# One level of Strassen's scheme for the three large products of a gated block

## The chip, the core and the metric

The kernel runs on one core of a Trainium2 chip. The metric is device time in microseconds (us), from the first to the last instruction of the program on that core. Five engines work side by side, each with its own queue of instructions in a fixed order: PE (TensorE, matrix products), DVE (VectorE), ACT (ScalarE), POOL (GpSimd) and SP (SyncE, which here issues DMAs). They wait for each other through semaphores. SBUF is the on-chip memory, PSUM the small memory into which PE accumulates, and DRAM is off the chip.

## The reference

One layer on 1024 positions and 2048 channels, all in float32:

```python
hn = rmsnorm(h, pre_g[l])
z = hn @ w_in[l]                                   # 2048 -> 5120
u, v, gate_a, xb, gate_b = jnp.split(z, splits, axis=-1)
ya = gmlp_branch(u, v, ...) * jax.nn.silu(gate_a)  # gelu(u) * (mix over positions of layernorm(gelu(v)))
yb = rglru_branch(xb, ...) * jax.nn.silu(gate_b)   # conv of width 4, two small gates, a linear recurrence
y = jnp.concatenate([rmsnorm(ya, gmlp_out_g[l]), rmsnorm(yb, lru_out_g[l])], axis=-1)
h = h + rmsnorm(y @ w_out[l], post_g[l])           # 2048 -> 2048
h = h + (p[l] @ w_pe[l]) * jax.nn.sigmoid(h @ w_pg[l])   # 2048 -> 2048
```

The three large products are those with `w_in`, `w_out` and `w_pg`.

## The kernel before

Channels lie on the 128 partitions and positions along the free axis. A float32 product is done as three passes of a shorter type, float32r: `split` (L71 to L79) makes of each operand a head (a rounding copy on ACT) and a rest (source minus head on DVE), and PE adds head by head, rest of the weights by head of the activations, and head of the weights by rest of the activations into one PSUM tile. Every full matmul has 128 x 128 weights and 512 positions.

`load_w` (L81) brings a tile of 128 x 512 weights from DRAM over SP's queue and splits it. `block` (L109) makes one block of 128 output channels: 16 blocks of K, three passes, two halves of the positions, so 96 matmuls into a PSUM tile of two banks. `group` (L155) does several blocks together, block of K by block of K, while the activations of a phase are still being made (`Stream`, L133). The activations of a phase stay in SBUF, split, for the whole phase (the pool `t4` of 47 tiles).

The phases are: A, the input projection (first three blocks of xb and gate_b in one `group`, then the recurrent branch `lru` block by block; the v blocks with positions on the partitions, L388 to L404; then u and gate_a); B, the output projection (`evac_o`, L481), whose result goes to DRAM; C, the residual sum and the gate product (`make_half`, L544, `finish`, L614). Before C the last block of B is done one half of the positions after the other (`block_by_cuts`, L119): the norm of the first half (`o_rms`, `o_spread`) stands in PE's order in the middle of the second half's products, and the first three blocks of C begin with the first half of six blocks of K (`early_h`, `N_STAGED`).

The code is recorded in the order of the text, and a scheduler then sets each engine's order by its own model of times. Counted in the built program, PE has 7218 matmuls' worth of 128 x 512 (two of 256 columns counted as one), beside some hundred small ones.

## Time and profile before

| | |
|---|---|
| median of 3 runs | 1708.62 us (1707.32 to 1708.95) |
| span of the profiled execution | 1707.4 us |
| PE, matmuls | 1679.2 us (98%) |
| PE, weight loads | 1383.9 us (81%) |
| DVE | 681.7 us (40%) |
| ACT | 493.0 us (29%) |
| POOL | 194.6 us (11%) |
| DMA | 139.67 MB, mean 82 GB/s |

A busy share is a mean over the span. What an engine that is idle on average costs is seen only in the stretch in which it is needed most, so the trace is also read by stretches of time. The granted clock is 1.00 where PE runs at 2.4 GHz and 0.50 at 1.2 GHz; a mean between them is a stretch with both.

### The profile page before, as it was taken

How to read it: one execution, taken by the hardware profiler on the slowest of the kernel's cores; microseconds unless marked ns; L12 is line 12 of the kernel's file. 1: busy time of each engine (PE TensorE's matmuls, PEld its weight loads, DVE VectorE, ACT ScalarE, POOL GpSimd, SP SyncE). 2: the span in 40 equal slices, each digit the busy share in tenths (PEclk: the TensorE clock that was granted, in tenths of full speed). 3: DMA queues.
4: the chain of work that ended last, by engine and by line, in shares of the span. 5: the costliest groups of instructions: out<-in, count | busy, mean ns of one | idle time of the engine just before them, and what ended most of it. 6: DMA issues, size and time to landing. Idle time of an engine off the chain costs nothing. (4 is left out here: it accounts for less than half of the span.)

```text
span 1707.4 us, 18341 instructions
## 1 busy us (share of the span) xinstructions
PE 1679.2 (98%) x7476; PEld 1383.9 (81%) x7476; DVE 681.7 (40%) x830; ACT 493.0 (29%) x666; POOL 194.6 (11%) x99
## 2 busy tenths in 40 slices
PE   7999999999999999999999999999999899999999
PEld 5888888888888888888888888888887588888887
DVE  7775455455343332222225731111118952221221
ACT  5554333345333222222223421111113321111110
POOL 5500000001000000000000111111111741111000
PEclk9999999999999999999999999999999999999999
DMA  6221111113323211111114032222237322221220
GB/s 219 91 72 53 65 65 62 64 60 117 87 80 99 78 40 50 50 49 46 48 50 147 21 109 71 73 74 74 74 124 275 134 93 74 75 76 57 74 75 25
DMA packets 66468, 139.67 MB, mean 82 GB/s; under 512 B 7376, under 2 KB 11600, under 8 KB 66384
## 3 DMA queue, kind: packets, MB, share of 16 engines
q1 hardware_dynamic: 60768, 118.52, 21.3%
q10 hardware_dynamic: 5616, 19.99, 3.0%
q8 instruction: 58, 0.95, 0.2%
q14 instruction: 26, 0.21, 0.0%
HBM read 118.03 MB, written 20.45 MB: 81 GB/s over the span
## 5 line engine op out<-in xcount | busy, mean ns | idle before, releaser
L106 PE MATMUL z<-xah,w_hl 128*128 128x512 f32 x2048 | 551.0, 392 | 11.7 <-ACT xah L77 7.9
L75 DVE TENSOR_TENSOR w_hl<-w_raw,w_hl 128x512 fp32r<-128x512 f32 (+2 forms) x339 | 259.2, 771 | 696.9 <-ACT w_hl L74 696.8
L74 ACT ACTIVATE w_hl<-w_raw 128x512 fp32r<-128x512 f32 (+2 forms) x339 | 206.9, 616 | 940.9 <-PE z L106 756.1
L106 PEld LDWEIGHTS z<-xah,w_hl 128*128 128x128 f32 x2048 | 385.9, 189 | 95.0 <-ACT xah L77 8.8
L106 PE MATMUL z<-xal,w_hl 128*128 128x512 f32 x1024 | 312.0, 391 | 0.0
L106 PE MATMUL z<-yah,w_hl 128*128 128x512 f32 x1024 | 272.2, 390 | 1.4 <-ACT yah L77 0.9
L106 PEld LDWEIGHTS z<-yah,w_hl 128*128 128x128 f32 x1024 | 191.9, 188 | 42.0 <-ACT yah L77 1.3
L106 PEld LDWEIGHTS z<-xal,w_hl 128*128 128x128 f32 x1024 | 193.0, 189 | 40.3
L106 PE MATMUL z<-hah,w_hl 128*128 128x512 f32 (+1 forms) x660 | 172.3, 385 | 5.0 <-DVE w_hl L75 5.0
L106 PE MATMUL z<-yal,w_hl 128*128 128x512 f32 x512 | 155.3, 389 | 0.0
L106 PEld LDWEIGHTS z<-hah,w_hl 128*128 128x128 f32 x660 | 123.0, 189 | 30.6 <-DVE w_hl L75 6.3
L106 PE MATMUL z<-hh,w_hl 128*128 128x512 f32 (+1 forms) x594 | 135.9, 386 | 2.8 <-ACT hh L74 2.8
L106 PEld LDWEIGHTS z<-hh,w_hl 128*128 128x128 f32 x594 | 110.1, 190 | 25.4 <-ACT hh L74 3.4
L106 PEld LDWEIGHTS z<-yal,w_hl 128*128 128x128 f32 x512 | 96.1, 188 | 20.0
L106 PE MATMUL z<-hal,w_hl 128*128 128x512 f32 (+1 forms) x330 | 101.8, 390 | 2.9 <-DVE hal L75 2.7
L397 PE MATMUL z<-w_hl,xah 128*128 128x512 f32 x256 | 100.0, 392 | 0.0
L399 PE MATMUL z<-w_hl,xal 128*128 128x512 f32 x256 | 99.8, 390 | 0.0
L398 PE MATMUL z<-w_hl,xah 128*128 128x512 f32 x256 | 99.8, 390 | 0.0
L231 POOL TENSOR_TENSOR acca<-acca,u 128x1024 f32<-128x1024 f32 x7 | 18.8, 2692 | 512.3 <-ACT u L230 512.3
L106 PEld LDWEIGHTS z<-hal,w_hl 128*128 128x128 f32 x330 | 62.4, 191 | 18.1 <-DVE hal L75 6.2
L231 POOL TENSOR_TENSOR acco<-acco,oq 128x1024 f32<-128x1024 f32 x14 | 33.6, 2398 | 288.8 <-ACT oq L230 288.8
L398 PEld LDWEIGHTS z<-w_hl,xah 128*128 128x128 f32 x256 | 48.1, 188 | 10.1 <-issue 0.2
(168 smaller groups left out, 1190.6 us busy)
## 6 DMA issues: line engine op xcount, KB each, us to landing
w_raw<-w_z SPq DMA_DIRECT2D x125, 256.0 KB, 3.0
w_raw<-w_v SPq DMA_DIRECT2D x64, 256.0 KB, 2.6
w_raw<-w_o SPq DMA_DIRECT2D x64, 256.0 KB, 3.1
w_raw<-w_g SPq DMA_DIRECT2D x64, 256.0 KB, 3.0
xr<-xT SPq DMA_DIRECT2D x25, 512.0 KB, 7.7
o_d<-o ACTq DMA_DIRECT2D x15, 512.0 KB, 2.9
outT<-sg ACTq DMA_DIRECT2D x15, 512.0 KB, 3.3
or<-o_d SPq DMA_DIRECT2D x9, 512.0 KB, 10.2
```

The source lines that it names most:

```text
L74: nc.scalar.activation(out=hi, in_=src, func=AF.Copy)
L75: nc.vector.tensor_tensor(out=lo, in0=src, in1=hi.bitcast(F32), op=ALU.subtract)
L106: nc.tensor.matmul(ps[:, c], lhsT=hl[:, w, j * P:(j + 1) * P], rhs=a[x][:, c], start=first and n == 0, stop=last and n == 2)
L231: nc.gpsimd.tensor_tensor(out=acc, in0=acc, in1=tmp, op=ALU.add)
L397: nc.tensor.matmul(ps, lhsT=xh, rhs=hl[:, 0], start=k == 0, stop=False)
L398: nc.tensor.matmul(ps, lhsT=xh, rhs=hl[:, 1], start=False, stop=False)
L399: nc.tensor.matmul(ps, lhsT=xl, rhs=hl[:, 0], start=False, stop=k == NK - 1)
```

## The change

Each of the products is cut in two along the output channels, the channels summed over, and the positions, and one level of Strassen's scheme (in Winograd's form) is used: seven products of half-size blocks in place of eight. A unit is a pair of blocks of 128 output channels (xb with gate_b, u with gate_a, the two halves of the output channels of B and C, and four units of v); a product of a unit ("a run") takes 8 blocks of K, three passes and 512 positions: 24 matmuls. There are 36 units, so 36 x 7 x 24 = 6048 matmuls of 128 x 512 where 6912 stood.

The seven products are done in two sets. Set 1 (`set1`) needs the activation quarters 11 and 21 and the sums T1 and T2; set 2 (`set2`) needs T3, T4 and quarter 22. All act tiles of one set fill the pool of activations (`N_ACT = 32` tiles), so a phase does set 1 for all units, then set 2. What set 2 still needs of set 1 goes to DRAM as partial sums (`u2`, `u4`, `c11`, `p7`, ...) and comes back. Normalised activations go to DRAM too (`xn_d`, `yn_d`, `h_d`) and are loaded again for each sum in which they stand (`fetch_x`, `fetch_y`, `fetch_h`) into a ring of four tiles (`t_ld`, `N_LD = 4`). The norm of x is now applied to x before the product. The product with `w_pe` moves to the start of the program, where x is loaded.

Units go through a set in groups of n = 1, 2 or 4 (the tuples `L1`, `U1`, `B1`, ...), each block of weights being split whole (128 x 1024). Weight sums are made on DVE and POOL from the raw tiles (`t_raw`, five of them). `load_late` makes a DMA wait for the first matmul of the run before the last recorded one.

```diff
+L1 = (1, 1, 1, 1, 4)
+ONES8 = (1,) * 8
+U1 = (2, 1, 1, 1, 1, 2)
+B1 = (4, 4)
+B2 = (2, 1, 1, 1, 1, 2)
+C1 = (4, 4)
+C2 = (2, 1, 1, 1, 1, 1, 1)
...
+    def load_late(out, src, back=2):
+        ins = load.dma_start(out=out, in_=src)
+        if len(marks) >= back:
+            tc.add_manual_dep(ins.ins, marks[-back].ins.name,
...
+        def t12(self, c):
...
+            x11, x12 = self.fetch(0, c), self.fetch(1, c)
+            sub(x11, x12, x11)
+            x22 = self.fetch(3, c)
+            sub(x22, x22, x11)
+            self.put("T2", c, x22)
+            self.put("T1", c, x11)
...
+        def t34(self, c):
...
+            x12, x22 = self.fetch(1, c), self.fetch(3, c)
+            sub(x12, x22, x12)
+            if ("T3", c) not in self.made:
+                self.put("T3", c, x12)
+            self.put("22", c, x22)
+            x11, x21 = self.fetch(0, c), self.fetch(2, c)
+            sub(x21, x21, x11)
+            sub(x21, x21, x12)
+            self.put("T4", c, x21)
...
+            for j in tiles:
+                for c in self.chunks(j):
+                    self.acts.t12(c)
+                x11 = a11[j] if self.n == 1 else self.raw(0, j)
+                a21, a22 = self.raw(2, j), self.raw(3, j)
+                add(a21, a21, a22)
+                sub(a22, a21, x11)
+                self.run(pa, "T2", self.hl(a22), j, False)
...
+            s3, a22 = [], []
+            for j in tiles:
+                for c in self.chunks(j):
+                    self.acts.t3(c)
+                a11, a21 = self.raw(0, j), self.raw(2, j)
+                sub(a11, a11, a21)
+                s3.append(a11)
+                self.run(pa, "T3", self.hl(a11), j)
+            self.each(p7, pa)
+            for j in tiles:
+                for c in self.chunks(j):
+                    self.acts.t34(c)
+                a22.append(self.raw(3, j))
+                self.run(pa, "T4", self.hl(a22[-1]), j, False)
+            self.each(p74, pa)
+            pb = [psum() for _ in tiles]
+            for j in tiles:
+                a12 = self.raw(1, j)
+                sub(a12, a12, a22[j], nc.gpsimd)
+                add(a12, a12, s3[j])
+                self.run(pb, "22", self.hl(a12), j)
+            self.each(p3, pb)
...
+    def fetch_h(q, c):
+        t = t_ld("h")
+        if (q, c) in normed_h:
+            load_late(t, h_d[q][c])
+            return t
+        normed_h.add((q, c))
+        i, j = q // 2, q % 2
+        x = t_ld("x2")
+        load_late(x, xq[q, c])
+        load_late(t, o_d[q][c])
+        for e in range(2):
+            nc.vector.scalar_tensor_tensor(out=t[:, e], in0=t[:, e],
+                                           scalar=col("post_g", 8 * i + 2 * c + e),
+                                           in1=s_o[j], op0=ALU.mult, op1=ALU.mult)
+        add(t, t, x, nc.gpsimd)
+        store.dma_start(out=h_d[q][c], in_=t)
+        return t
...
+    for j in range(2):
+        s_o[j] = norm_half([acco[:, HALF[j]], *last_sq[j]], D, "s_o", j)
```

What moves in the engines' orders is seen at three places.

PE in the recurrent stage, before: L106 is a block product (`xah`, `xal` are head and rest of the activations), L336 the small gate products of `lru`. A block's 96 matmuls end in a PSUM tile of its own, and the next block has another.

```order
L106 MATMUL z<-xah,w_hl 128x512 x2
L336 MATMUL g<-xcl,wgs 128x512 x2
L336 MATMUL g<-xch,wgs 128x512 x2
L106 MATMUL z<-xah,w_hl 128x512 x2
L106 MATMUL z<-xal,w_hl 128x512 x2
L106 MATMUL z<-xah,w_hl 128x512 x4
L106 MATMUL z<-xal,w_hl 128x512
```

PE in the recurrent stage, after: the end of a run with T3, then four matmuls of the run with quarter 22 (`a22h`, `a22l`), then the run with T4, which adds into the PSUM tile that T3 filled and that has been read in between.

```order
L282 MATMUL z<-aT3h,w_hl 128x512 x2
L282 MATMUL z<-aT3l,w_hl 128x512
L282 MATMUL z<-a22h,w_hl 128x512 x2
L282 MATMUL z<-a22l,w_hl 128x512
L282 MATMUL z<-a22h,w_hl 128x512
L282 MATMUL z<-aT4h,w_hl 128x512 x2
L282 MATMUL z<-aT4l,w_hl 128x512
```

Between the reading of T3's sum and the first matmul of T4 there are now four matmuls of other work; before, no product went back into a tile that had been read.

PE between B and C, before: L199 sums squares over the partitions, L216 spreads the norm's scale; both stand among products (`yah` of B's last block, `hh` of C's first blocks).

```order
L106 MATMUL z<-hh,w_hl 128x512 x27
L199 MATMUL g<-ones_r,oq 128x1
L199 MATMUL g<-ones_r,acco 128x1
L199 MATMUL g<-ones_r,oq 128x1
L199 MATMUL g<-ones_r,acco 128x1
L199 MATMUL g<-ones_r,oq 128x1
L199 MATMUL g<-ones_r,acco 128x1
L199 MATMUL g<-ones_r,oq 128x1
L106 MATMUL z<-hh,w_hl 128x512 x21
L216 MATMUL g<-diag,ones_r 128x512 x2
L106 MATMUL z<-hh,w_hl 128x512 x54
```

PE between B and C, after: L155 and L172 do the same work, for the first half of the positions and then for the second, and the products of C (`a11h`) come behind both.

```order
L172 MATMUL g<-diag,ones_r 128x512 x2
L155 MATMUL g<-ones_r,acco 128x1
L155 MATMUL g<-ones_r,sq 128x1 x4
L155 MATMUL g<-ones_r,acco 128x1
L155 MATMUL g<-ones_r,sq 128x1 x4
L155 MATMUL g<-ones_r,acco 128x1
L155 MATMUL g<-ones_r,sq 128x1 x4
L155 MATMUL g<-ones_r,acco 128x1
L155 MATMUL g<-ones_r,sq 128x1 x4
L172 MATMUL g<-diag,ones_r 128x512 x2
L282 MATMUL z<-a11h,w_hl 128x512 x8
```

No block product stands between the two halves' norms any more; the same pattern stands ahead of U1 and of B.

DVE at the beginning of C, before (halves of 512 positions: scale L545, sum L548, rest L75):

```order
L545 SCALAR_TENSOR_TENSOR xo<-xo,cv,g 128x512 x2
L548 TENSOR_TENSOR xo<-xo 128x512 x2
L545 SCALAR_TENSOR_TENSOR xo<-xo,cv,g 128x512
L75 TENSOR_TENSOR hh<-xo,hh 128x512 x2
L548 TENSOR_TENSOR xo<-xo 128x512
L545 SCALAR_TENSOR_TENSOR xo<-xo,cv,g 128x512 x2
L75 TENSOR_TENSOR hh<-xo,hh 128x512
```

DVE in set 1 of C, after, from the T1 and T2 sums of the first four units (L877 scales o, L121 is a difference or a rest):

```order
L877 SCALAR_TENSOR_TENSOR h<-h,cv,s_o 128x512 x2
L121 TENSOR_TENSOR h<-h 128x1024
L121 TENSOR_TENSOR w_hl<-w_raw,w_hl 128x1024
L877 SCALAR_TENSOR_TENSOR h<-h,cv,s_o 128x512 x2
L121 TENSOR_TENSOR w_hl<-w_raw,w_hl 128x1024
L121 TENSOR_TENSOR h<-h 128x1024
L121 TENSOR_TENSOR aT2l<-h,aT2h 128x1024
L121 TENSOR_TENSOR aT1l<-h,aT1h 128x1024
```

This stands there for each of four chunks of K, beside the weight sums; the sum of x and o between L877 and L121 moved to POOL (16 additions of 128 x 1024).

## Rows read from the trace of the kernel before

**Rows 1.** The page, busy time of each engine, share and instructions.
```profile
PE 1679.2 (98%) x7476; PEld 1383.9 (81%) x7476; DVE 681.7 (40%) x830; ACT 493.0 (29%) x666; POOL 194.6 (11%) x99
```

**Rows 2.** Stretches: us, busy (instructions) PE, PEld, DVE, ACT, POOL, granted clock, DMA share, GB/s.
```profile
0.00:24.00 24.00, 16.12 (x59) 12.44 (x60) 16.25 (x41) 14.17 (x20) 7.39 (x9) 1.00 0.76 260
100.00:300.00 200.00, 200.00 (x879) 164.18 (x878) 105.00 (x106) 89.80 (x110) 9.65 (x4) 1.00 0.20 66
```

**Rows 3.** Groups by shape: out<-in, shapes, count | busy us, mean ns | idle before, releasers.
```profile
L231 POOL TENSOR_TENSOR acco<-acco,oq 128x1024 f32<-128x1024 f32 x14 | 33.6, 2398 | 288.8 <-ACT oq L230 288.8
...
L352 DVE TENSOR_TENSOR_SCAN q<-r,i 128x1024 f32<-128x1024 f32 x8 | 18.3, 2288 | 0.2
...
L462 ACT ACT_TABLE_LOAD x8 | 10.3, 1283 | 9.4 <-DVE u L309 9.3
...
L75 DVE TENSOR_TENSOR xcl<-xc,xch 128x1024 fp32r<-128x1024 f32 x8 | 9.8, 1220 | 1.4 <-ACT xch L74 1.3
...
L545 DVE SCALAR_TENSOR_TENSOR xo<-xo,cv,g 128x512 f32<-128x512 f32 x12 | 8.6, 743 | 2.3 <-PE g L216 2.3
...
L74 ACT ACTIVATE xch<-xc 128x1024 fp32r<-128x1024 f32 x8 | 8.4, 1047 | 3.7 <-DVE xc L319 3.7
...
L548 DVE TENSOR_TENSOR xo<-xo 128x512 f32<-128x512 f32 x12 | 7.9, 685 | 0.0
```

**Rows 4.** Timeline near the start: start us, us, engine, line, operation, tiles.
```profile
23.34 9.34 POOL L231 TENSOR_TENSOR accx<-accx,xr 128x1024 f32<-128x1024 f32 x3
...
27.62 6.21 DVE L75 TENSOR_TENSOR w_hl<-w_raw,w_hl 128x512 fp32r<-128x512 f32 x3
...
34.95 0.68 DVE L75 TENSOR_TENSOR w_hl<-w_raw,w_hl 128x512 fp32r<-128x512 f32 x1
```

**Rows 5.** Timeline of the second norm before C, and DVE after it.
```profile
1296.51 0.58 ACT L503 ACTIVATE oq<-z 128x512 f32<-128x512 f32 x1
...
1297.72 0.28 PE L199 MATMUL g<-ones_r,oq 128*128 128x1 f32 x2
...
1301.73 0.69 DVE L214 TENSOR_TENSOR diag<-ident,sp_lo 128x512 fp32r<-128x512 f32 x1
...
1313.51 0.68 DVE L75 TENSOR_TENSOR hh<-xo,hh 128x512 fp32r<-128x512 f32 x1
1314.11 0.69 DVE L548 TENSOR_TENSOR xo<-xo 128x512 f32<-128x512 f32 x1
```

**Rows 6.** Stretches of the step from B to C, columns as in Rows 2.
```profile
1300.00:1310.00 10.00, 7.24 (x27) 5.62 (x26) 7.29 (x16) 1.59 (x4) 0.00 (x0) 0.87 1.04 398
...
1320.00:1330.00 10.00, 8.83 (x38) 6.54 (x36) 10.00 (x10) 3.53 (x7) 7.82 (x5) 1.00 1.03 409
...
1350.00:1360.00 10.00, 4.96 (x15) 3.07 (x15) 10.00 (x8) 2.18 (x4) 8.66 (x6) 0.76 0.29 93
```

**Rows 7.** DMA issues: tensors, queue, count, KB each, median us to landing.
```profile
w_raw<-w_z SPq DMA_DIRECT2D x125, 256.0 KB, 3.0
...
xr<-xT SPq DMA_DIRECT2D x25, 512.0 KB, 7.7
...
or<-o_d SPq DMA_DIRECT2D x9, 512.0 KB, 10.2
...
pr<-pT SPq DMA_DIRECT2D x2, 512.0 KB, 6.3
```

More of the change, by code (lines that the diff above doesn't have):

```diff
@@ new lines, in groups, with __init__, p1, p2 @@
+    def groups(w, sizes, acts):
+        at = 0
+        for n in sizes:
+            yield at, Group(w[at:at + n], n, acts)
+            at += n
+    class First1:
+        def __init__(self, d, at, done, turned=False):
+            self.d, self.at, self.done, self.t = d, at, done, {}
+        def p1(self, u, ps):
+            self.t[u, 1] = t_h("c11")
+            copy(self.t[u, 1], ps)
+        def p2(self, u, ps):
+            t = self.t[u, 1]
+            add(t, t, ps)
+            self.done(self.at + u, t)
+        def u2(self, u, ps):
+            self.t[u, 2] = t_h("u2")
+            copy(self.t[u, 2], ps)
+            store.dma_start(out=self.d[self.at + u]["u2"], in_=self.t[u, 2])
+        def u4(self, u, ps, b):
+            t = t_h("u4")
+            if b is None:
+                copy(t, ps)
+            else:
+                add(t, self.t[u, 2], b)
+            store.dma_start(out=self.d[self.at + u]["u4"], in_=t)
+        def run(self, group):
+            group.set1(self.p1, self.p2, self.u2, self.u4)
@@ new lines, in block_kernel @@
+    for n in range(4):
+        if n:
+            we_raw.append(t_raw())
+            load.dma_start(out=we_raw[n], in_=w_e[n])
+        for qc in order[6 * n:6 * n + 6]:
+            load_x(*qc)
+        hl = pool.tile([P, 2, T], F32R, tag="hl", bufs=N_HL, name="w_hl")
+        split(hl[:, 0], hl[:, 1], we_raw[n])
+        for qc in order[6 * n:6 * n + 6]:
+            square_x(*qc)
+        if n == 3:
+            norm_x()
+        for b in range(4 * n, 4 * n + 4):
+            pss = [psum(), psum()]
+            for k in range(2):
+                o = ((b - 4 * n) * 2 + k) * P
+                for i, (w, x) in enumerate(((0, 0), (1, 0), (0, 1))):
+                    for j, ps in enumerate(pss):
+                        nc.tensor.matmul(ps, lhsT=hl[:, w, o:o + P], rhs=pa[k][x][:, j],
+                                         start=k == 0 and i == 0, stop=k == 1 and i == 2)
+            for j, ps in enumerate(pss):
+                t = t_h("pe")
+                copy(t, ps)
+                store.dma_start(out=pe_d[b % 8][:, 2 * (b // 8) + j], in_=t)
@@ new lines, in block_kernel, with fetch_y @@
+    ax3 = Acts(fetch_x)
+    for at, g in groups(w_u1, U1, ax3):
+        ls = [LastU(at + n) for n in range(g.n)]
+        each = [lambda n, *a, k=k: getattr(ls[n], k)(n, *a) for k in ("p1", "p2", "u2", "u4")]
+        g.set1(*each)
+    s_a = {}
+    normed = set()
+    def fetch_y(q, c):
+        t = t_ld("y")
+        if (q, c) in normed:
+            load_late(t, yn_d[q][c])
+            return t
+        normed.add((q, c))
+        load_late(t, y_d[q][c])
+        i, j = q // 2, q % 2
+        s = s_a[j] if i else s_b[j]
+        for e in range(2):
+            nc.vector.scalar_tensor_tensor(out=t[:, e], in0=t[:, e],
+                                           scalar=col("gmlp_out_g" if i else "lru_out_g", 2 * c + e),
+                                           in1=s, op0=ALU.mult, op1=ALU.mult)
+        store.dma_start(out=yn_d[q][c], in_=t)
+        return t
@@ new lines, in block_kernel, with done_o @@
+    acca = acc
+    acc = cpool.tile([P, T], F32, tag="acco", name="acco")
+    o_u = parts("ou", NH, ("u2", "u4"))
+    started = set()
+    def done_o(u, q, t, last=None):
+        store.dma_start(out=o_d[q][u // 2][:, u % 2], in_=t)
+        j = q % 2
+        if last is not None:
+            sq = t_h("sq")
+            nc.scalar.activation(out=sq, in_=t, func=AF.Square)
+            last.setdefault(j, []).append(sq)
+            return
+        add_sq(acc[:, HALF[j]], t, j not in started)
+        started.add(j)
@@ new lines, in block_kernel, with done_z @@
+    acco = acc
+    z_u = parts("zu", NH, ("u2", "u4"))
+    def done_z(u, q, t):
+        ph = t_ld("ph")
+        load_late(ph[:, 0], pe_d[u][:, q])
+        load_late(ph[:, 1], h_d[q][u // 2][:, u % 2])
+        nc.scalar.activation(out=t, in_=t, func=AF.Sigmoid)
+        mul(t, t, ph[:, 0])
+        add(t, t, ph[:, 1])
+        store.dma_start(out=outq[q, u], in_=t)
+    for j in range(2):
+        s_o[j] = norm_half([acco[:, HALF[j]], *last_sq[j]], D, "s_o", j)
+    ah1 = Acts(fetch_h)
+    for at, g in groups(w_g1, C1, ah1):
+        First1(z_u, at, lambda u, t: done_z(u, 0, t)).run(g)
@@ L644 @@
+    ah2 = Acts(fetch_h)
+    for at, g in groups(w_g2, C2, ah2):
+        Last2(z_u, at, g.n, done_z).run(g)
 def kernel(**inputs):
```

942 lines of the change are left out of this document (493 added, 449 removed).

## The prediction

> **What bounds the kernel now.** I read the busy row of the page first: PE is busy for 1679.2 of 1707.4 us, DVE for 681.7, ACT for 493.0, POOL for 194.6 [rows 1]. The whole idle time of PE is 28.2 us, at the start and at the step from B to C [rows 2, 6]. So the time is the number of matmuls times their pace, and nothing else is worth much by itself. The pace is seen in a stretch without a hole: 879 matmuls in 200 us [rows 2], 0.2275 us each at full clock. The other engines have slack on the mean, but the change spends just that slack, so the second reading is what their operations cost: a DVE operation on two tiles of 128 x 1024 takes 1.22 us, on 512 columns 0.685, a scaling of 512 columns 0.743, the same sum on POOL 2.4, a copy on ACT 1.05 and a change of ACT's function table 1.28 [rows 3]. The third is whether DVE and POOL can work at once: near the start POOL makes three sums in 9.34 us, and in the same time three DVE operations that take 0.68 alone take 6.21 together [rows 4]. From 27.62 to 33.83 us there are 2.0 us of DVE's own work and two POOL sums of 2.4: they add up to 6.8 of the 6.2 us. Where both read two SBUF tiles I therefore add DVE's and POOL's times instead of taking the longer.
>
> **What it removes.** Of 6912 block matmuls 6048 stay; 864 x 0.2275 = 196.6 us of PE. PE's own work after is 1679.2 - 196.6 = **1482.6 us** (the product with `w_pe`, the gates and the norms are in it as before). This is the floor; before's idle 28.2 us are replaced by the terms below. A run of 24 matmuls is 5.46 us.
>
> **What it adds.** Weight rests go from 4 to 7 per unit of 128 x 1024, with four weight sums on DVE and one on POOL; over the program DVE comes to some 1100 us by these rows and POOL to some 210. On the mean that fits under PE; by stretches it doesn't always. ACT comes to some 850 us (256 weight copies of 1.05, 79 table loads, 285 DMA issues); no stretch is bound by it beside the start.
>
> *Start, +22.* PE begins with the product with `w_pe`: half a MB of p lands in 6.3 us [rows 7] and is copied, so at about 8.5 us where before began at 5. It has 192 matmuls, 43.7 us, of which 144 stand ahead of the norm of x and 48 behind. The norm needs all of x: with p and `w_e` 11.5 MB, 44 us at the 260 GB/s of the first stretch [rows 2] or 29 at 400 [rows 6]. Then come two norm chains (5.3 us each, next term) and the 48 matmuls, 10.9: the first run begins between 63 and 69 us, 19 to 26 after PE's own work. I take 22.
>
> *Norms in the open, +40.* Before, the squares' sum begins at 1297.72 us and the last diagonal ends at 1302.42 [rows 5]; with the spreading matmuls and a copy 5.3 us, hidden beside products. After, no product stands between, and the second half's chain begins only behind the first's. Ahead of U1: 2 x 5.3 = 10.6. Ahead of C: the last sum and square (0.69 + 0.58) [rows 3, 5] and both chains, 11.9. Ahead of B the first half's chain can run beside the last run, but the last units must first be gated: two sums, two table loads, two functions, three products, a square and a POOL sum, 9.3 us, some 2.5 more for the second unit of that group, then one chain: 17. If only one chain shows each time it is 28, with cold buffers 50.
>
> *First groups of a set, +81.* Here the activation sums and rests of a set must be made while its first runs go. I count DVE against PE, in us. Set 1 of v and of B: 32 scalings, 8 activation sums, 16 activation rests, 16 weight rests, 8 weight sums, 8 additions of 0.69, in all 88 against 16 runs of 87.4, but 54 of it against the 43.7 of the T runs: +3 and +5. Set 1 of C: 8 more for outputs, 96, and 16 sums on POOL, 38.4: 134 against 87.4, **+47**, the largest single term. Set 2 of v: 40 operations, 49, and 9.6 on POOL against 43.7: +15. Set 2 of B and C: the first two units take 28 activation operations, 10 for weights and 6 additions (18 in C), with POOL 58 and 64 against 32.8: +25 and +31. The T runs of the first two units of u: 29 against 21.8: +8. Together 134. Two things take from it. Part of set 2 can be done beside the last runs of set 1, where DVE is half idle; `load_late` lets loads start two runs, 10.9 us, ahead: three times 11, 33. And operations that follow each other closely start 0.60 us apart where one takes 0.68 [rows 5]: 0.07 for some 300 operations, 20. That leaves 81. Below, 35: only C's remains and half of it is hidden. Above, the whole 134.
>
> *Recurrent stage, +10.* A pair of units has 10 operations of 1.22 for weights and some 23 of 0.7 with two scans for the gates (a scan of 1024 takes 2.29 [rows 3], so 1.15 each): 31.4 on DVE and 7.2 on POOL, 38.6 against 156 matmuls, 35.5. The first two pairs also make the mix: 44.5 against 39.3. Eight pairs: +29; with the closer starts (2.8 a pair) +7. I take 10, bounds 0 and 29.
>
> *Turning a PSUM tile round, +12.* Some 40 times PE adds into a tile that has just been read out. The reading is 0.69 or 0.6, the waits at both ends some tenths, and four matmuls stand between, 0.91. An estimate of 0.3 each; 5 if they hide it, 30 if the reader is often in the middle of a 1.22 us operation, since it stands in the same queue as the rests.
>
> *Clock, +8, and the end, +3.* After the two holes before, the granted clock was 0.87 and 0.76 in 10 us [rows 6], one to two us lost each time. With some dozen holes and half of them in stretches where PE isn't the bound, 8 (bounds 3 and 20). At the end four operations of 512 columns stand where 256 columns stood.
>
> *Queues.* A `load_late` that waits holds back the weight loads behind it on SP. Weights take 3.0 us to land, activations 7.7 to 10.2 under load [rows 7], and both are ordered some 10.9 us ahead: hidden, costed at nothing; if the cover is gone, 3 us for each of 24 chunks, 72. Stores wait on ACT's queue for DVE or POOL, with weight copies behind them; three raw weight tiles ahead hide that. Traffic goes from 140 to some 390 MB, 235 GB/s on the mean, with 43 MB in C's first group: 107 us at 400 GB/s, less than the 134 of DVE and POOL. The trace shows 409 GB/s for ten us [rows 6]. The Trainium skill, page "DMA: Bandwidth & Descriptors", section "Where 436 GB/s comes from", says that transfers from HBM are bound at about 358 GB/s per core; no stretch here bears that out, and by it (an estimate) C's first group would move its bytes in 120 us and B's in 90, which would add some 5 us in B to the sum.
>
> **The sum.** 1482.6 + 22 + 40 + 81 + 10 + 12 + 8 + 3 = 1658.6 against the profiled 1707.4; the median of the runs lies 1.2 above the span, so **1660 us**, 3% faster. Loss of PE: 176 us where before had 28. The change is even when the terms reach 224.8.
>
> **The rivals.**
> Slower: *DVE and POOL behind one port become the bound.* Place: first groups and the recurrent stage. If the in-order queue of DVE lets nothing be done ahead and every operation costs its full row, the first groups cost 134 and the pairs 29: +72, 1732. It decides from 49 us over my sum. For it: rows 4, and that PSUM readings stand in the same queue. Against: DVE half idle beside the last runs of each set 1.
> Slower too: *SP's queue.* Late loads hold weights back: +72, 1732 likewise; it would be seen as waits for DMA rather than for DVE. Against: the loads of rows 7 land within two runs.
> Faster: *the cover holds.* First groups 35, pairs 0, turns 5: 1660 - 46 - 10 - 7 = 1597. For it: the scheduler has already put set 2's first T3 rests ahead of the end of set 1.
> That the change doesn't do what it says is out: 6048 matmuls stand in the built order.
>
> **How the numbers follow.** Forecast (1625 to 1703) 0.48, port 0.20, SP 0.07, cover 0.25. Range 1595 to 1745: both rivals' times with a little for the norms and the start. A measurement tells about 0.2% from no change. Faster: 0.25 and nearly all of the forecast's, 0.70; the two slower rivals with a part of them near even: 0.25 slower, 0.05 the same.
>
> **What would show it.** PE busy near 1480 with some 170 us idle. C's first 16 runs should take 105 to 125 us, set 2's first groups 45 to 50, a recurrent pair 36 to 38, each norm a hole of 10 to 17. Waits of PE should name DVE and ACT on `w_hl` and on the activations. Wrong if a pair takes 40 or more, if holes lie in the long groups of single units, or if DMA is what PE's feeders wait for.

## The result: 8.5% slower, and the profile after

The changed kernel takes 1853.6 us (median of three runs, 1849.6 to 1859.7) where the kernel before took 1708.6: a ratio of 1.085, 95% interval 1.082 to 1.089. The forecast was 1660 us, its range 1595 to 1745. The removal of 864 matmuls is real, yet the time rose by 145 us. The page of the changed kernel, to be held against [rows 1]: the busy row, then PE's busy tenths and the granted clock in 40 slices of 46.3 us.

```profile
span 1851.9 us, 18321 instructions
...
PE 1568.2 (85%) x6612; PEld 1266.4 (68%) x6612; DVE 1161.1 (63%) x1340; ACT 723.5 (39%) x884; POOL 236.9 (13%) x125
...
PE   7699999989888898867999789988987425997888
...
PEclk9799999999998999978999789999997867998999
```

PE is idle for 283.7 us; before it was 28.2. And its busy time is 1568.2, where the forecast's floor was 1482.6: 85.6 us more for the same matmuls, because the slices with holes are also slices with a lower clock (7 and 6 in the last row). A hole is paid twice, once as a wait and once in the slow matmuls behind it. No other engine is near full; DVE is at 63%.

What PE waited for (us in total, times, longest):

```profile
PE z L282 <- ACT aT2h L130: 98.5, 10, 35.2
PE g L172 <- DVE diag L170: 49.5, 7, 11.6
PE g L687 <- ACT xch L130: 26.8, 6, 5.7
PE z L282 <- DVE w_hl L121: 18.6, 12, 4.3
```

These are the T2 activations of set 1, the diagonals of the norms, the inputs of the gates (`xch` is the head of the convolution's result), and only then the weight rests. To find where they lie I cut the trace at the first matmul of each stage. A pair is set 2 of one recurrent unit and of one unit of u with gate_a; the first two pairs also make the mix over positions. The table has each stage's matmuls times 0.2275 us, what the forecast makes of the stage (gross, before its 53 us for work done ahead), the measurement, and the measurement in the last experiment below. All in us.

| stage | PE alone | forecast | changed | last experiment |
|---|---|---|---|---|
| start, to v's first run | 43.7 | 63 to 69 | 84.9 | 85.8 |
| set 1 of v | 87.4 | 90 | 91.7 | 90.5 |
| set 1 of the recurrent units | 174.7 | 174.7 | 174.4 | 174.4 |
| set 2 of v | 65.5 | 80 | 82.9 | 70.9 |
| two pairs with the mix | 78.6 | 79 to 89 | 108.3 | 92.8 |
| six pairs | 213.0 | 216 to 228 | 260.6 | 214.4 |
| norm ahead of U1 | 0 | 10.6 | 20.6 | 1.6 |
| U1, first group | 43.7 | 52 | 58.3 | 73.8 |
| U1, rest | 131.0 | 131 | 132.0 | 135.7 |
| norm ahead of B | 0 | 17 | 22.9 | 0.2 |
| B set 1, first group | 87.4 | 92 | 104.8 | 116.0 |
| B set 1, second group | 87.4 | 87.4 | 87.0 | 87.3 |
| B set 2 | 131.0 | 156 | 154.7 | 152.5 |
| norm ahead of C | 0 | 11.9 | 26.0 | 10.3 |
| C set 1, first group | 87.4 | 134 | 181.0 | 133.7 |
| C set 1, second group | 87.4 | 87.4 | 87.0 | 87.1 |
| C set 2 | 131.0 | 162 | 175.0 | 168.2 |

The windows of five of these in the changed kernel (columns as in [rows 2]):

```profile
176.60:351.00 174.40, 174.40 (x769) 143.86 (x768) 74.20 (x68) 46.98 (x55) 4.80 (x2) 1.00 0.51 167
...
542.10:803.00 260.90, 230.20 (x938) 183.26 (x937) 181.71 (x238) 161.13 (x205) 42.73 (x23) 0.93 0.48 151
...
803.00:823.40 20.40, 5.07 (x22) 4.08 (x21) 17.11 (x29) 8.33 (x13) 2.37 (x1) 0.57 0.47 149
...
1463.70:1589.90 126.20, 51.74 (x193) 41.17 (x194) 58.56 (x59) 22.14 (x25) 21.45 (x8) 0.72 0.53 186
1589.90:1676.90 87.00, 87.00 (x385) 72.06 (x384) 51.69 (x52) 28.40 (x33) 2.12 (x1) 1.00 0.73 261
```

The first and the last row are stages whose activations lie ready: PE has no hole at all, with DVE at 43% and 59%. The six pairs (second row) lose 30 us to holes and 17 to the clock at DVE 70%. The fourth row is the T part of C's first group, its eight runs with T2 and T1: 126 us for 44 us of matmuls, with DVE busy 46% and POOL 17%. So in neither bad stretch is an engine full. Nor are DVE and POOL full if their times are added, as the forecast adds them: 224.4 us in the 260.9 of the six pairs, 80.0 in the 126.2 of the T part. The question for the runs is what else holds these stretches.

**A pair, read by instruction.** DVE, ACT and PE between the end of a recurrent unit's third run (691.5 us) and its gates, word for word from the timeline (start, duration, engine, line, operation, tiles, and in brackets the idle time before it and what ended it):

```profile
692.32 1.22 DVE L124 TENSOR_TENSOR w_raw<-w_raw 128x1024 f32<-128x1024 f32 x1 [2.83 <-POOL w_raw L121]
693.46 0.68 DVE L124 TENSOR_TENSOR xb<-xb,z 128x512 f32<-128x512 f32 x1
694.06 1.22 DVE L121 TENSOR_TENSOR w_hl<-w_raw,w_hl 128x1024 fp32r<-128x1024 f32 x1
...
696.05 0.54 DVE L625 TENSOR_SCALAR xc<-xb,cv 128x512 f32<-128x512 f32 x1
...
699.08 1.23 DVE L121 TENSOR_TENSOR w_raw<-w_raw 128x1024 f32<-128x1024 f32 x1 [1.15 <-DMA w_raw<-w_u]
...
701.48 0.74 DVE L628 SCALAR_TENSOR_TENSOR xc<-xb,cv,xc 128x512 f32<-128x512 f32 x1
```

```profile
702.26 0.63 ACT L130 ACTIVATE xch<-xc 128x512 fp32r<-128x512 f32 x1
702.80 0.58 ACT L130 ACTIVATE p<-z 128x512 f32<-128x512 f32 x1
```

```profile
702.94 0.88 PE L687 MATMUL g<-xch,wgs 128*128 128x512 f32 x2 [4.42 <-ACT xch L130]
```

The convolution needs five short operations, some 3.5 us. They are spread over 9 us: ahead of them stands a weight operation that waited for POOL, and between them stand two more, one of which waited for a load, and operations of the first half's gates. One run of 24 matmuls, 5.6 us, covers this on PE; the chain from the run's end to the gates is 11.4 us. Note the ACT row behind xch: ACT copies T3's sum `p`, for which the next run waits, only after xch.

**C's T part, read the same way.** SP's loads, the scaling on DVE, the sum on POOL and the first T2 matmul:

```profile
1472.28 0.33 SPq L197 DMA_DIRECT2D h<-h  x1
...
1485.25 0.33 SPq L197 DMA_DIRECT2D h<-o  x1
```

```profile
1481.34 1.41 DVE L877 SCALAR_TENSOR_TENSOR h<-h,cv,s_o 128x512 f32<-128x512 f32 x2 [3.68 <-DMA h<-o]
...
1489.83 1.42 DVE L877 SCALAR_TENSOR_TENSOR h<-h,cv,s_o 128x512 f32<-128x512 f32 x2 [3.35 <-DMA h<-o]
...
1496.54 1.23 DVE L121 TENSOR_TENSOR h<-h 128x1024 f32<-128x1024 f32 x1 [5.30 <-DMA h<-h]
```

```profile
1482.88 2.34 POOL L124 TENSOR_TENSOR h<-h,x 128x1024 f32<-128x1024 f32 x1 [26.50 <-DVE h L877]
```

```profile
1498.91 1.65 PE L282 MATMUL z<-aT2h,w_hl 128*128 128x512 f32 x3 [35.23 <-ACT aT2h L130]
```

PE stops at 1463.7. The first load of h is issued only at 1472.3, the third at 1485.3, right when POOL has finished its sum and so let a tile go: load, scaling, sum, next load, one after the other through a ring of four tiles (`t_ld`).

### The profile page after: what moved, and what is told of

It is laid out like the page before. It is cut to its first block, busy times and chain, and to the rows that moved or that the text cites. A ratio compares the mean times of both kernels' runs of the same rounds, so it can differ in the third digit from the quotient of the medians.

```text
span 1851.9 us, 18321 instructions
## 1 busy us (share of the span) xinstructions
PE 1568.2 (85%) x6612; PEld 1266.4 (68%) x6612; DVE 1161.1 (63%) x1340; ACT 723.5 (39%) x884; POOL 236.9 (13%) x125
## 5 line engine op out<-in xcount | busy, mean ns | idle before, releaser
L130 ACT ACTIVATE w_hl<-w_raw 128x1024 fp32r<-128x1024 f32 x256 | 269.9, 1057 | 545.6 <-PE z L282 422.5
L121 DVE TENSOR_TENSOR w_hl<-w_raw,w_hl 128x1024 fp32r<-128x1024 f32 x256 | 318.2, 1247 | 143.6 <-ACT w_hl L130 142.6
L282 PE MATMUL z<-aT2h,w_hl 128*128 128x512 f32 x512 | 146.5, 413 | 95.9 <-ACT aT2h L130 95.9
L124 DVE TENSOR_TENSOR w_raw<-w_raw 128x1024 f32<-128x1024 f32 x72 | 103.5, 1438 | 154.4 <-POOL w_raw L121 95.0
L121 POOL TENSOR_TENSOR w_raw<-w_raw 128x1024 f32<-128x1024 f32 x36 | 88.7, 2463 | 838.7 <-DMA w_raw<-w_v 321.2
L282 PE MATMUL z<-aT4h,w_hl 128*128 128x512 f32 x512 | 170.6, 421 | 25.2 <-DVE c L124 13.0
L282 PEld LDWEIGHTS z<-aT2h,w_hl 128*128 128x128 f32 x512 | 102.0, 201 | 121.3 <-ACT aT2h L130 99.7
L282 PE MATMUL z<-aT3h,w_hl 128*128 128x512 f32 x512 | 158.3, 397 | 18.3 <-DVE carry L707 13.2
L282 PE MATMUL z<-a22h,w_hl 128*128 128x512 f32 x512 | 161.2, 397 | 10.9 <-DVE w_hl L121 9.4
L282 PE MATMUL z<-a11h,w_hl 128*128 128x512 f32 x512 | 141.2, 399 | 0.0
L282 PE MATMUL z<-a21h,w_hl 128*128 128x512 f32 x512 | 136.1, 390 | 4.9 <-ACT a21h L130 3.4
L282 PE MATMUL z<-aT1h,w_hl 128*128 128x512 f32 x512 | 136.9, 391 | 1.1 <-DVE p L124 1.1
L282 PEld LDWEIGHTS z<-a22h,w_hl 128*128 128x128 f32 x512 | 97.7, 191 | 34.7 <-DVE w_hl L121 11.9
L121 DVE TENSOR_TENSOR w_raw<-w_raw 128x1024 f32<-128x1024 f32 x72 | 92.0, 1278 | 26.1 <-DMA w_raw<-w_o 8.3
```

What stands on the lines that cost most here:

```text
L121: (engine or nc.vector).tensor_tensor(out=out, in0=a, in1=b, op=ALU.subtract)
L124: (engine or nc.vector).tensor_tensor(out=out, in0=a, in1=b, op=ALU.add)
L130: nc.scalar.activation(out=out, in_=src, func=AF.Copy)
L282: mm = nc.tensor.matmul(ps, lhsT=l, rhs=r, start=fresh and kp == 0 and n == 0, stop=kp == 7 and n == 2, skip_group_check=True)
```

## The experiments

Each starts from the changed kernel (1853.6 us) if nothing else is said; times are medians, compared with it (the kernel before took 1707.5 to 1708.5 us beside them). Where a stage is given, it is read from one profiled execution of the run.

**1. Gates one run later, by the program's order.**

```diff
                 store.dma_start(out=self.d[k], in_=t)
-                do_later()
+                if k != "p7":
+                    do_later()
```

> Edit: in the recurrent stage the gate matmuls of a unit's second half are put behind the second run of the gelu unit (24 matmuls more between the convolution and the gates); nothing else. Changed kernel: 1853.6 us, pairs 41 to 56 us, 369 us for all eight against 291.6 us of PE at full clock; six waits for xch, 26.8 us. Theory A (the chain convolution, split, gates is longer than the one run of 5.5 us that covers it, and each hole is paid a second time in half clock): the six holes of 4 to 7 us and the slow T4 runs behind them go, pairs 37 to 39 us, 45 to 65 us less in all, 1790 to 1810 us. Theory B (DVE is saturated in this stage, by its in-order wait on POOL's weight sums among others): the hole only moves to the next run that needs DVE, pairs 41 us or more, within 10 us of 1853.6.

Measured: 1878.4 us, 25 us slower; the later pairs 45 to 48 us. Neither theory. The trace says why: the order on the engines is not that of the program. Two of the six gate matmuls still stood ahead of T4 (PE waited up to 6.9 us there), and on DVE the chain had moved behind more weight work. The run didn't test what it was made for.

**2. The finished outputs of C's first group later, out of the ring.**

```diff
             t = self.t[u, 1]
             add(t, t, ps)
-            self.done(self.at + u, t)
+            if not self.late:
+                self.done(self.at + u, t)
 
         def u2(self, u, ps):
+            if self.late:
+                self.done(self.at + u, self.t[u, 1])
```

> Edit: in the first group of set 1 of C the four c11 outputs are finished behind the T runs and not ahead of them, so that their loads of the p product and of h (tiles ph) do not fill the ring of four load tiles before the T activations are fetched; nothing else. Changed kernel: the T part of that group takes 126.2 us for 43.7 us of PE, its largest hole 35.2 us. Theory A (the ring of four is held by ph, and the fetch of h begins only when it is let go): the hole of 35 us shrinks to 12 to 18 us, the T part to 95 to 105 us, 20 to 40 us less in all, 1815 to 1835 us. Theory B (16 POOL sums of 2.4 us beside DVE, 134 us of work for the whole group): the group still takes 165 to 181 us, within 10 us of 1853.6.

Measured: 1840.0, 13.7 less. T part 110.0 for 126.6, largest hole 17.2 for 35.2: the hole is in theory A's range, but the T part (95 to 105) and the whole (20 to 40 less) miss it. The mechanism is theory A's, with about half of its gain. The four columns now take 25 us each, and in them SP waits for POOL 36 us to get tiles (first row below).

**3. POOL's weight differences on DVE.**

```diff
-                    sub(a12, a12, a22, nc.gpsimd)
+                    sub(a12, a12, a22)
```

> Edit: the 36 weight differences that POOL makes (2.4 us each) are made by DVE (1.22 us each); nothing else. In the changed kernel DVE waits 95 us for them in its own queue, 29 times, 5.2 us the longest. Theory A (exposed chains in the order of the program): the recurrent stage's holes wait for a convolution behind these waits, so a part goes: 10 to 30 us less, mostly in the pairs, C's first group unchanged (it has none of them). Theory B (DVE and POOL shut each other out, and the stage is bound by their sum): DVE gains 29 waits of 3 us and 36 x 1.2 us, pairs fall to 37 or 38 us, 30 to 60 us less. If neither matters, within 10 us of 1853.6.

Measured: 1820.7, 33 less: theory B's range by its size, but not in its place. 11 us come from v's second set, 5 each from those of B and C, and only 8 from the pairs; the six fall from 260.6 to 254.4, 42.4 us each. So POOL's differences cost time, whether through clashes with DVE or because DVE waits for them in its queue, which this run doesn't separate; but they aren't what makes the pair long.

**4. The sums of h with x on DVE.**

```diff
-        add(t, t, x, nc.gpsimd)
+        add(t, t, x)
```

> Edit: the 16 sums of h with x in the fetch of C's first group are made by DVE (1.22 us) and not by POOL (2.4 us); nothing else. C's first 16 runs take 181 us against 87.4 us of PE. Theory A (ring of four held by ph, then a serial chain of load, scaling, sum and load): the chain is 1.2 us shorter a step, 16 steps, 5 to 15 us less, the hole of 35 us becomes 28 to 33. Theory B (POOL's 38 us and DVE's 96 us add up behind one port): 134 us of work becomes 115, the group gives back 19 us or more, with the clock 20 to 35 us less.

Measured: 1843.9, 9.7 less; norm ahead of C and first group 198.5 for 206.7. The hole is 34.0. A shorter step in the same serial chain (theory A).

**5. Gates pinned behind T4 on PE.** An order edge to the last matmul of the run, so that PE's order is what the text says.

```diff
+            ends[:] = [mm]
...
-                do_later()
+                if k != "p7":
+                    with tc.issue_after(ends[0].ins):
+                        do_later()
```

> Edit: the gate matmuls of a unit's second half are pinned on PE behind the last matmul of the gelu unit's second run (T4), so that 48 matmuls, 11 us, and not 24 stand between the run whose sum the convolution needs and the gates; the run before this one left the first two gate matmuls ahead of T4 and so did not test it. In the changed kernel the gates' input is ready 11.4 us after that run (691.5 to 702.9 us) and PE waits 4.4 us, then runs 24 matmuls in 7.3 us for 5.6. Theory A (the place of the gates alone): the wait goes, pairs 37 to 39 us, 30 to 50 us less in all. Theory B (DVE's queue is the bound: the chain waits behind weight rests and POOL sums, and gates that come later push the next unit's chain back): pairs 41 us or more, 1840 us or more.

Measured: 1862.8, 9 slower, pairs 44 us. Theory B by the numbers, but not by its reason. PE's largest wait in the six pairs, and ACT ahead of it:

```profile
PE z L283 <- ACT p L130: 33.0, 6, 5.7
```

```profile
660.12 0.63 ACT L700 ACTIVATE th<-th 128x512 f32<-128x512 f32 x1
660.78 0.63 ACT L130 ACTIVATE xch<-xc 128x512 fp32r<-128x512 f32 x1
661.32 0.58 ACT L130 ACTIVATE p<-z 128x512 f32<-128x512 f32 x1
```

The gates no longer stop PE, but T4 adds into the PSUM tile that holds T3's sum, and ACT copies that sum only after its part of the recurrent chain. The wait has gone from PE's queue to ACT's.

**6. The norms beside products.** The recurrent output's norm is made behind U1's first group, that of the gelu output behind two runs of B, those of B beside its last runs and behind three runs of C:

```diff
-    s_b = [norm_half([acc[:, c]], D // 2, "s_b", j) for j, c in enumerate(HALF)]
...
         g.set1(*each)
+        if not s_b:
+            s_b = [norm_half([accb[:, c]], D // 2, "s_b", j) for j, c in enumerate(HALF)]
```

> Edit: the three norm chains between the products are made later or earlier, beside products: that of the recurrent output behind the first group of U1, those of the gelu output behind two a11 runs of B, that of B's first half beside the last a22 runs of B and that of its second half behind three a11 runs of C. The same work, in another place. Changed kernel: 20.3, 22.7 and 25.7 us between the last matmul before and the first after. Theory A (they are holes because nothing is ordered beside them, and the clock adds to each): the three stretches fall to a few us each, 50 to 65 us less in all, 1790 to 1805 us. Theory B (the work of the next group, scaling and rests, has to follow the chain, so the hole moves into the first group): these come down but the first groups of U1, B and C grow by 10 us or more each, 15 to 30 us less in all.

Measured: 1840.8, 12.9 less. The three holes went from 69.5 to 0.6 us, and 52 came back: U1's first group +20.8, B's +16.3, B's last groups +14.6. Theory B. A part is PE's order again, one wait in U1's first group:

```profile
PE g L172 <- DVE diag L170: 11.3, 1, 11.3
```

**7. Summing and spreading of each norm a run or more apart**, by order edges on top of 6.

```diff
+    def norm_sum(accs, n):
...
+            with tc.issue_after(ends[0].ins):
+                rms_small(accs, n, small)
...
+    def norm_spread(small, name):
...
+            with tc.issue_after(ends[0].ins):
+                spread(small, dst)
```

> Edit: the norms beside products as in the run before of that name, and besides the spreading matmuls of each half are pinned a run or more behind its summing matmuls, so that PE does not stand before them. In that run the three stretches between products fell from 69.5 to 0.6 us, but U1's first group grew by 20.8 us, of which 11.3 were one wait of PE for a diagonal, B's first half by 16.3 and B's last groups by 14.6. Theory A (PE's order was the reason for the return): of the 52 us given back 25 to 45 go, 1790 to 1815 us. Theory B (DVE has that work to do anyhow and the groups are bound by it): the groups keep their growth, 1830 to 1845 us.

Measured: 1833.1, 7.7 less than 6. Of 52 us given back some 8 are won: norm and first group together take 67.5 us for U1 (78.9 in the changed kernel, 79.3 in 6), 113.9 for B (127.7, 121.3). The rest stays, as theory B has it. A reading that fits, but that no run tests by itself: while PE stood at the norm, DVE and the loads had been preparing the next group.

**8. x of C's first group out of the ring**, on top of 2: two dead tiles of 4 KB take the loads of x.

```diff
-        x = t_ld("x2")
+        if q == 0:
+            x = t_ld("x2")
+        else:
+            nx.append(q)
+            x = cpool.tile([P, 2, TH], F32, tag=("acc", "acco")[len(nx) % 2], name="x2")
```

> Edit: that of the late outputs, and in C's first group the loads of x for the second, third and fourth quarter go to two tiles of 4 KB whose former contents are dead by then, so that the ring of four load tiles holds only h. With the late outputs alone the T part of the group took 110.0 us against 126.6, its four columns 25.4 us each, SP waiting 35.7 us for POOL to let tiles go. Theory A (the ring is the bound: a serial chain of load, scaling, POOL sum, difference and the next load): columns 15 to 20 us, the T part 65 to 85 us, the whole 45 to 65 us below 1853.6. Theory B (DVE and POOL): columns stay at 23 us or more, T part 100 us or more, 10 to 25 us below.

Measured: 1810.6, 43 less than the changed kernel, 29 less than 2. T part 85.5 us. SP's waits for POOL in the T part, of run 2 and of this one, with the windows of this one and of the changed kernel (above) alike in everything but time:

```profile
SPq L197 <- POOL h L124: 35.7, 8, 5.8
```

```profile
SPq L197 <- POOL h L124: 9.7, 3, 5.2
```

```profile
1455.50:1540.90 85.40, 51.72 (x194) 40.52 (x193) 57.37 (x55) 23.97 (x27) 16.77 (x6) 0.82 0.76 263
```

DVE's work in it is 57.4 us, in the changed kernel it was 58.6, in 126 us. With the outputs out of the way and two more tiles the same work takes 41 us less, so the ring of tiles held these 41 us. It isn't bandwidth either: the same loads now run at 263 GB/s, where they ran at 186. By its numbers the run lies just outside theory A (65 to 85 us, 45 to 65 less in all). What holds the 85 us that are left it doesn't say: in the whole first group, 136.8 us now, DVE is busy 96.9 and POOL 42.7, together the whole time.

**9. Runs 3, 4, 6 and 8 together.**

> Edit: four of the edits together: POOL's weight differences and the sums of h with x on DVE, the norms beside products, and the ring of C's first group unloaded as in the run before. If their places do not overlap, the gains add: 33 for the weight differences, 5 for the sums, 50 to 65 for the norms, 45 to 65 for the ring: 1690 to 1720 us, near the kernel before (1708.6). If they are one resource seen from four sides (DVE), they do not add and the sum stays above 1750 us.

Measured: 1766.0. That is above 1750, where the expectation put "one resource seen from four sides"; but its sum was made with gains of 133 to 168 us, and the runs by themselves give 33 + 10 + 13 + 43 = 99. Of these 99 us 88 come together, so they nearly add.

**10. ACT's rounding copy behind its copy of T3's sum**, on top of 5:

```diff
-            split(xch, xcl, xc)
-            later.append(lambda: self.rest(j, g, xc, xch, xcl))
+            def parts():
...
+                split(xch, xcl, xc)
+                later.append(lambda: self.rest(j, g, xc, xch, xcl))
+            if j == 0:
+                parts()
+            else:
+                later.append(parts)
...
+                ins = nc.scalar.activation(out=t, in_=ps, func=AF.Copy)
+                with tc.issue_after((ins if k == "p7" else ends[0]).ins):
+                    do_later()
```

> Edit: the gates behind T4 as in the run before, and besides, on ACT, the rounding copy of the second half's convolution (xch) is put behind the copy of T3's sum to SBUF (p), for which T4 waits; in that run ACT did xch first, stood still for DVE's convolution, and T4 waited 5.7 us a pair for p, 27.3 us in five pairs. Pairs took 44 us. Theory A (in-order queues of ACT and PE pass DVE's convolution chain of 11 us on to T4; with both taken out of the way it is covered): pairs 37 to 39 us, 1800 to 1825 us in all. Theory B (DVE's work in the pair is the bound): pairs stay at 41 us or more, and the wait goes to weights or sums of the next unit.

Measured: 1840.9, 12.8 less than the changed kernel and 22 less than 5. The last six pairs take 39 to 42 us, between the theories. xch wasn't all that stood ahead of `p`.

**11. Runs 3, 4, 7, 8 and 10 together.**

> Edit: both of the above with POOL's weight differences and sums of h with x on DVE and the ring of C's first group unloaded. Without the two pinned orders the sum of the other four took 1766.0 us. If the pinned orders work, 30 to 50 us less from the pairs and 25 to 45 from the norms: 1671 to 1711, at or below the kernel before (1708.5). If DVE is the bound of pairs and groups, 1750 us or more.

Measured: 1734.6, 119 less than the changed kernel, 1.5% above before (interval 1.2% to 1.9%), between the two theories. T4 still waits 23.9 us for `p` in eight pairs.

**12. T4 in a PSUM tile of its own**, on top of 11: PE need not wait for ACT's copy, and DVE adds the two sums.

```diff
             self.each(p7, pa)
+            if apart:
+                pa = [psum() for _ in tiles]
...
-                self.run(pa, "T4", self.hl(a22[-1]), j, False)
+                self.run(pa, "T4", self.hl(a22[-1]), j, apart)
```

> Edit: the sum of the run before, and in the gelu units T4 adds into a PSUM tile of its own, so that it need not wait until ACT has copied T3's sum; DVE adds the two (0.69 us) where ACT copied. In the run before T4 still waited for that copy, 23.9 us in eight pairs, because ACT stood for a square (P0, P1) or for DVE's product (the others) ahead of it. Theory A (in-order queues): T4 starts at once; the first two pairs fall from 54.5 and 51.6 to 43 to 46 us, the others from 41 to 38 to 40, 25 to 35 us less than 1734.6: 1700 to 1710. Theory B (DVE, 79% busy in this stage, is the bound): the wait goes to the gates or the next unit, 1725 us or more.

Measured: 1710.2, level with before (ratio 1.002, 1.000 to 1.003). Pairs 38.1 us, those with the mix 50.3 and 44.8.

**13. The gates behind U's third run as well, and the norm of x spread over the last w_pe matmuls.** The gates' line of 10 now says `"p3"`, so 72 matmuls and not 24 stand before the gates, 11 us more; at the start 48 of the 192 matmuls are split around the norm.

> Edit: as the one before, with the gates behind the third run of the gelu unit (33 us more matmuls between than the first kernel had: 72 and not 24), and at the start 48 matmuls of the product with w_pe stand between the sums of the norm of x and its spreading. Theory A: no pair waits for gates, the later six at 37 to 38 us; the start falls from 77.1 to 66 to 70 us; 1685 to 1702 us. Theory B: the gates' chain, put 17 us later, holds the next unit's sums on DVE and pairs stay at 40 us or more; the start alone gives 7 to 10 us.

Measured: 1702.2. The six pairs, 215.2 us in one window, beside all that PE waited for in it:

```profile
518.80:734.00 215.20, 213.18 (x931) 174.12 (x930) 193.69 (x253) 157.47 (x200) 23.66 (x12) 1.00 0.56 179
```

```profile
PE z L296 <- DVE gb L124: 1.9, 5, 0.7
```

PE runs without a hole at full clock while DVE is busy 193.7 of 215.2 us, 90%. With 70% in the changed kernel it had holes of 30 us. DVE's work by itself was never the bound of this stage. The start gained nothing: counted from PE's first matmul it takes 75.1 us, but v's first set 95.0; with the start unchanged they take 76.9 to 79.0 and 88.3 to 91.7 in the runs above.

**14. The order alone**, with T4 in its own PSUM tile as in 12, in the changed kernel with POOL's differences left where they were.

> Edit: in the changed kernel as it stood, the order of the recurrent stage alone: T4 of the gelu unit in its own PSUM tile, ACT's rounding copy of the convolution behind its copy of T3's sum, the gates of the second half behind the third run of the gelu unit. POOL keeps its weight differences. In the sum of all edits with this order the six pairs without the mix take 36.0 us each (35.5 of matmuls), with DVE 90% busy. Theory A (the order in the queues alone cost it): these six pairs 36 to 38 us, all eight 310 to 325 instead of 369, 1795 to 1812 us. Theory B (POOL's differences on DVE were needed too, since DVE waits for them in its queue): six pairs of 39 us or more, 1820 us or more.

Measured: 1813.1, 40.5 less. All eight pairs take 320.9 us for 368.9, the six 228.6, 38.1 each: at the border between the theories. Some 7 us come back at the norm ahead of U1 (27.3 us for 20.2). The window of the six pairs, to be held against that of the changed kernel (260.90) above:

```profile
537.60:765.00 227.40, 205.26 (x890) 166.54 (x888) 188.74 (x236) 157.55 (x199) 43.72 (x22) 0.98 0.53 170
```

So 32 of the 47.6 us that the six lose to PE's own 213.0 go by order and the second PSUM tile, with more work on DVE and as much on POOL; order edges alone gave 16 of them (run 10, 244.6). What is left is near the forecast's own sum for a pair, 38.6: DVE and POOL are busy 188.7 + 43.7 = 232.5 us in these 227.4. With the differences on DVE and the other edits that sum falls (193.7 + 23.7 = 217.4 us in run 13), and another 14 us go (214.4 in the next run). So what is left may be DVE's and POOL's times added, as the forecast had it; no run tests that alone.

**15. Run 13 with the start of the changed kernel.**

> Edit: the sum of all edits with the late gates, but the start as in the changed kernel. With 48 matmuls between the sums of the norm of x and its spreading, start and first set of v together took 75.1 + 95.0 us, without 77.1 + 89.0. Theory A (that edit lost 4 us): 1694 to 1700 us. If the start does not matter: 1702 us.

Measured: 1700.0, a ratio to the kernel before of 0.996 (0.994 to 0.997). Runs 13 and 15 are the two versions that come out below the kernel before, by 0.4% each. The times of the two overlap (1691.5 to 1710.7 and 1696.2 to 1703.7), so the question about the start stays open.

```profile
span 1695.3 us, 18218 instructions
...
PE 1539.0 (91%) x6612; PEld 1247.1 (74%) x6612; DVE 1203.1 (71%) x1400; ACT 719.6 (42%) x877; POOL 111.9 (7%) x73
```

DVE has 42 us more to do than in the changed kernel, and the kernel is 154 us faster. C's first group in it, where POOL has no work any more:

```profile
1306.30:1440.00 133.70, 105.27 (x426) 85.45 (x427) 98.48 (x111) 39.67 (x46) 0.00 (x0) 0.85 0.82 290
```

## Why the prediction was wrong, step by step

*What was right.* 6048 block matmuls stand and PE's pace is 0.2275 us where activations lie ready: the second groups of set 1 and the recurrent units' set 1 ran without a hole. Set 1 of v (90) and the gross figures for the second sets of v and B (80 and 156) came out at 91.7, 82.9 and 154.7. DVE comes to 1161 us, forecast 1100; the traffic is the 390 MB of the forecast.

*What was wrong, in us over PE's own work.* The forecast's terms come to 176. By the table the stages lose 41 at the start, 69.5 at norms, 77 in the pairs and 215 in the groups and sets: 403. The difference is 227; 33 of it are in the floor already (1482.6 is that much above the matmuls counted here, for norm matmuls and slow stretches of before). That leaves the 194 us by which the time missed.

- **Recurrent stage, 10 forecast, 77 measured.** The step that failed is "31.4 on DVE and 7.2 on POOL, 38.6 against 156 matmuls": a sum of work against a sum of work, as if it were all that a pair can cost. The pairs had holes with DVE at 70% and ran at PE's pace with DVE at 90%. What was missing is the dependence of three in-order queues: PE waits for ACT, ACT stands behind an operation of the recurrent chain, and that behind DVE, where weight work that isn't urgent stands between five short operations. That cost 48 us in eight pairs, which run 14 took away (368.9 to 320.9). The sum itself came close to what is left then: 29.3 us over PE's 291.6, where the forecast's bound above was 29. Its own sign, "wrong if a pair takes 40 or more", came true. The Trainium skill, page "Perfetto Trace Analysis", section "Identifying the Most-Contended Engine", looks for the engine with the highest occupancy and optimizes it first. Occupancy alone doesn't show the cause here: at 70% of DVE the six pairs had 30 us of holes, at 90% none over 0.7 us.
- **C's first group, 47 forecast, 94 measured.** What failed is again the sum taken as the whole cost: "134 against 87.4". The group took 181.0. A ring of four tiles, filled by loads for outputs that nobody waited for, made the work serial, and that has no term in the prediction, which counted the raw weight tiles and never the load tiles. With the ring relieved (run 8) the group takes 136.8, near the 134 of the forecast, with the 16 sums and the scalings all still there. Whether DVE and POOL together hold it there is open. In run 15 the group takes 133.7 us with POOL at nothing and DVE at 98.5, though with a part of B's norm in it. The rival that gave SP's queue 0.07 had the place in part: SP stood, and DVE waited for loads (`h<-o` 29.3 us, `h<-h` 18.0 in this group), which was the forecast's last sign of being wrong. But SP stood for tiles, 43.7 us for POOL to let them go, and not because loads were set late.
- **Work done ahead and closer starts, 53 taken off the first groups.** They didn't come. The first groups and second sets (without C's first group) lose 121 us, the gross figure was 87. Runs 6 and 7 show that a group grows when the norm's hole ahead of it goes: part of the work ahead was done in those holes, it seems, and not beside the last runs.
- **Norms, 40 forecast, 69.5 measured.** For each diagonal PE waited 4 to 12 us, where the whole chain had been put at 5.3: between the small operations of the chain DVE makes rests and scalings of the next group; ahead of U1 the last unit's gating was left out, though the same was counted ahead of B; and with the clock at 0.57 the runs around the hole pay too.
- **Clock, 8 forecast, some 86 measured** (it is contained in the stages above). The price of a hole, one to two us, was right in C's T part (51.7 us busy for 43.7, four holes) and low in the pairs (17 us in six holes). In the pair shown the six gate matmuls behind the hole are busy 2.8 us for 1.5 and T4 takes 7.3 for 5.6, at granted clocks of 0.56 and 0.76. The number of holes was wrong too: "some dozen", when PE has 54 of over 1 us. The Trainium skill, page "TensorE: Matmul & The Clock Gate", section "HAM oscillation — how this bites in real kernels", describes a kernel that pays the slow clock again at each wait of its loop; the rows agree, with a granted clock of 0.72 in C's T part.
- **Turning a PSUM tile, 12 forecast.** In the changed kernel PE waits some 14 us for a reader of a PSUM tile (13.0 for DVE's `c`, 1.1 for `p`), near the forecast. The larger part was hidden behind the gates: with these moved away, T4 waits 33.0 us for ACT's copy (run 5).
- **Start, 22 forecast, 41 measured.** PE waits from 48.0 us for the squares (to 51.9) and then for the two chains, which end at 72.8, where the forecast had 55 or so. The one try to cover it (run 13) gained nothing in all.
- **The port.** DVE and POOL do shut each other out: of 585 DVE operations on two tiles of 1024 in the changed kernel 54 overlap a POOL sum by over 0.3 us, and their median is 2.1 us for 1.22, some 40 us of DVE's time over the whole program. Run 3 gives 33 us back, in which the 95 us that DVE stood in its queue for POOL's differences (29 waits) have a share of their own. So this rival, with 0.20 of chance, had the right sign and at most about a sixth of the miss.

The slower rival's price, 1732, was still 120 us short, so the range missed as well: it was built from the same sums of work. The 5 us that the forecast would have added in B by the bandwidth that it cites don't follow from its numbers, 90 us against the 92 of its gross term.

*Open.* What holds the first groups of U1 and B (73.8 for 43.7 and 116.0 for 87.4 us in run 15; in B's DVE is busy 88.4 us and POOL 8.4). Their T activations are made from the same ring of four tiles, but no run relieved it there. And whether a start exists that covers the norm of x.

## What to carry to other kernels

When a change removes work from the bounding engine and adds it to engines with slack, cost the chains besides the sums: follow one output through every in-order queue between two matmuls, and ask what stands ahead of each step and how many tiles its ring has. An order that the program's text gives is a wish; look at the order on the engine before believing an experiment on it (runs 1 and 5). And count each hole on PE with the slow run behind it.

## What the runs showed of the hardware that I had not expected

PE kept full clock and had no hole over 0.7 us with DVE busy 90% of 215 us (run 13): an in-order engine at 90% can feed PE if what is urgent stands in front. And one hole of 4.4 us in the changed kernel cost 3 us more behind it: the six gate matmuls were busy 2.8 us for 1.5, and the 24 of T4 ran at 0.305 us each and not at 0.23.
